# Fewer adaLN blocks in the last group of down-projections, and a joint visit of the value products and the reciprocal broadcasts

## The chip, the cores and the metric

One NeuronCore of a Trainium2 chip runs the whole program. The metric is device time in microseconds, the median of the runs. TensorE (PE) multiplies, VectorE (DVE) and ScalarE (ACT) do the element-wise work, GpSimd (POOL) helps, SyncE (SP) issues most DMAs. Each engine works through its own queue in order; semaphores tie the engines together.

## The reference

One step of a trunk of four layers on 640 tokens (128 of context, 512 latent), width 1024, in fp32. Layer i mixes tokens by kind i mod 3: attention (layers 0 and 3), a Conformer convolution (layer 1), a gated linear attention, GLA (layer 2). A gated ConvFFN with 2816 hidden channels follows in every layer. Each sub-layer is an RMSNorm with shift, scale and gate from `silu(cond) @ mod_w + mod_b`, one set for the context tokens and one for the latent ones:

```
sh1, sc1, g1, sh2, sc2, g2 = split(silu(cond) @ mod_w[i] + mod_b[i], 6)
x = x + g1 * mixer(rms_norm(x, norm1_g[i]) * (1 + sc1) + sh1)
h = rms_norm(x, norm2_g[i]) * (1 + sc2) + sh2
u = dwconv3(h @ w_up + b_up)                 # a, g = halves of u
x = x + g2 * ((silu(g) * a) @ w_down + b_down)
```

In attention a latent query reads its 8x16 neighbourhood and 256 cached context keys, a context query the 128 context keys; the softmax is divided by its sum at the end, 16 heads of 64.

## The kernel before, in words

**Order.** The program is a list of tasks, each with the weights it needs (`units`). `run` works through it in order, and every engine's queue gets its instructions in that order. `weave(main, extra, rate)` puts further tasks between the main ones: after each main task that has units it adds `rate` to a count, and for each whole 1 it takes one task of `extra`. The count starts at 0 in each call.

**Weights.** `fill` issues the loads on SP into a ring of four tiles of 128x1024. `advance` turns them, half by half, into an upper part (ScalarE, L170) and a lower part (on VectorE in the ConvFFN, L171), into rings of four halves, so about two weights ahead of their use. A unit of kind "m" is no weight for TensorE: when `advance` comes to it, it calls `row_unit` at once. That is one **adaLN block**: two VectorE instructions (L377), which multiply 128 rows of `mod_w` by the two condition vectors and sum, for one of the eight row tiles of one of the six vectors of the next layer. `rows_tasks` lists 24 of them (scale 1, shift 1 and gate 2 of the next layer) for the ConvFFNs of layers 0, 1 and 2. Layer 3 has none.

**Matrix products.** `proj` does per step of k six matmuls (L224 to L229: upper and lower parts, two halves of the tokens). In the middle and at the end it calls `advance`, and after every step `pump`, which lets one step of lane A (every generator in it) and one of lane B (its first generator) issue their work. If a step of lane A says "ax", lane B is left out.

**ConvFFN.** `ffn` has three groups of up-projections (10, 7 and 5 pairs of up tasks), each followed by a group of eight down-projection columns over 8, 7 and 7 chunks of hidden channels (`GRP`). In the last group the evacuations are flushed first, then columns 0 and 1 run interleaved as one task, then columns 2 to 7. Each column ends in `x_update`: VectorE adds the gated result to x (L596), then `fin` writes upper (ScalarE, L263) and lower part (VectorE, L266) of the next layer's input, and squares are summed for its norm (ScalarE L287, GpSimd L289). With the next layer an attention, the latent rows are written in a permuted order. `RATES` are the two weave rates, for the ups and for the downs; the first four up tasks stand ahead of the weave, and in layer 0 four more tasks with units (its own gate 2) are among the first ups.

**Attention.** Per pair of heads three projections (q, k, v, 8 steps each) run through `proj`. Lane A holds their evacuations: `normed` for q and k, `values` for v, which transposes the values into the PSUM banks `SB` and `PB` (L802) and has ScalarE copy them out (L803, L804), and says "ax". Lane B holds `units`, the softmax of a pair: scores into `SB`, exponentials with their sums into R, transposes in `PB` (`trans`), products with the values into `B6` (`pv`, L884), for the context tokens into `PB` (L902). At the end the reciprocals of R are broadcast over partitions by ten products with the identity into `SB` and `PB` (L910), copied out by ScalarE (L913, L914), and multiplied in by VectorE (L920). The next pair's `units` start when its keys are done.

Of the kernel before, what the change touches and what calls it, by code (L numbers as in the profile page):

```python
# [25 lines left out]
P = 128  # L26
NCH = 8
CTX = 128
LAT = 512
TOK = CTX + LAT  # L30
# [7 lines left out]
KA = 5  # L38
MODW = 8
W2 = 2  # L40
RATES = (0.0, 1.3)
GRP = ((0, 8), (8, 15), (15, 22))
EPS = 1e-6
EXPLN = "natural_log_exp_and_others"
# [81 lines left out]
class Trunk:  # L126
# [351 lines left out]
    def ffn(self, layer):  # L478
# [152 lines left out]
        def add_down(q):  # L631
            lo, hi = GRP[q]
            main.append(Task(self.lane_a.drain))
            unit = lambda j: ("w", self.i["w_down"][layer, j, :, lo * P:hi * P])
            if q == 0:
                main.append(Task(prep_gb))
            j0 = 0
            if q == 2:
                main.append(Task(flush))
                if nxt:  # L640
                    main.append(Task(lambda: self.shift_cols(self.mod[(layer + 1) % 2][0][:])))
                j0 = 2
                main.append(Task(lambda *ws: down(ws, [0, 1], q), [unit(0), unit(1)]))
            for j in range(j0, NCH):
                main.append(Task(lambda w, j=j: down([w], [j], q), [unit(j)]))
# [4 lines left out]
        for q, (lo, hi) in enumerate(GRP):  # L650
# [3 lines left out]
            if q == 0:  # L654
                tasks += main[:4]
                main = self.weave(main[4:], early, 0.4)
            tasks += self.weave(main, extra, RATES[0], False)
            main = []
            add_down(q)
            tasks += self.weave(main, extra, RATES[1], q == 2)  # L660
            main = []
# [4 lines left out]
    def attention(self, layer, la):  # L666


        S = type("S", (), {})()
# [37 lines left out]
        def load_bias(p, i):  # L707
            at = S.nb % 2
            S.nb += 1
            self.nc.sync.dma_start(out=S.bias[:, 1 + 2 * at:3 + 2 * at], in_=self.i["bias"][la, p, i])  # L710
            S.at[p, i] = 1 + 2 * at
# [97 lines left out]
        def softmax(sc, st, bias, parts, R):  # L809

            nc = self.nc
            sm = self.sm.next()
            n = sc.shape[-1]
            if bias is not None:
                nc.vector.tensor_tensor_reduce(out=st.rearrange("p (a b) -> p a b", a=2),
                                               in0=sc.rearrange("p (a b) -> p a b", a=2), in1=bias, scale=1.0,
                                               scalar=-3.0e38, op0=ALU.add, op1=ALU.max, accum_out=sm[:, 0:1])
                src = st
            else:
                nc.vector.tensor_reduce(out=sm[:, 0:parts], in_=sc.rearrange("p (a b) -> p a b", a=parts),  # L820
                                        axis=AX_X, op=ALU.max)
                src = sc
            nc.vector.tensor_scalar(out=sm[:, 2:2 + parts], in0=sm[:, 0:parts], scalar1=-1.0, scalar2=None,  # L823
                                    op0=ALU.mult)
            w = n // parts
            for a in range(parts):
                nc.scalar.activation(out=st[:, a * w:a * w + w], in_=src[:, a * w:a * w + w], func=AF.Exp,  # L827
                                     bias=sm[:, 2 + a:3 + a], accum_out=R[:, a:a + 1])

        def units(p):  # L830

            nc = self.nc
            b = S.bufs[p]
            Q, K, V, Vc = b["Q"], b["K"], b["V"], b["Vc"]
            sts, pts = {}, {}
            R = S.R.next()

            def scores(n):
                st = self.T.next()[:, 0:512]
                sts[n] = st  # L840
                if n == 8:
                    sc = S.SB[:, 0:256]
                    for hd in range(2):
                        o = KH * hd + 896
                        for part in range(2):
                            nc.tensor.matmul(sc[:, P * hd:P * hd + P], Q[:, hd, part, 0:CTX], K[:, o:o + P],
                                             start=(part == 0), stop=(part == 1))
                    softmax(sc, st[:, 0:256], None, 2, R[:, 8:10])
                else:
                    i, hd = n // 2, n % 2  # L850
                    o = KH * hd
                    sc = S.SB[:]
                    s = 256 + P * i
                    rhs = K[:, o:o + 2 * s].rearrange("p (a b) -> p a b", a=2)[:, :, 0:256]
                    q0 = CTX + P * i
                    nc.tensor.matmul(sc, Q[:, hd, 0, q0:q0 + P], rhs, start=True, stop=False)
                    nc.tensor.matmul(sc, Q[:, hd, 1, q0:q0 + P], rhs, start=False, stop=True)
                    at = S.at[p, i] + hd
                    softmax(sc, st[:], S.bias[:, 0:at + 1:at], 1, R[:, n:n + 1])

            def finish(n):
                if n < 8 and n % 2 == 1:
                    i = 4 * p + n // 2 + 2
                    if i < 4 * NCH:
                        load_bias(i // 4, i % 4)

            def trans(n):
                st, pt = sts.pop(n), S.PT.next()
                m = 2 if n == 8 else 4
                for c in range(m):  # L870
                    nc.tensor.transpose(S.PB[:, P * c:P * c + P], st[:, P * c:P * c + P], self.ident[:])
                if n % 2:
                    nc.vector.tensor_copy(out=pt[:, 0:P * m], in_=S.PB[:, 0:P * m])
                else:
                    nc.scalar.copy(out=pt[:, 0:P * m], in_=S.PB[:, 0:P * m])
                pts[n] = pt

            def pv(i):
                a, c = pts.pop(2 * i), pts.pop(2 * i + 1)
                blocks = (Vc[:, 0], Vc[:, 1], V[:, 1 + i], V[:, 1 + (i + 1) % 4])  # L880
                for k in range(4):
                    for hd, pt in ((0, a), (1, c)):
                        r = slice(64 * hd, 64 * hd + 64)
                        nc.tensor.matmul(S.B6[r, P * i:P * i + P], blocks[k][:, r], pt[:, P * k:P * k + P],  # L884
                                         start=(k == 0), stop=(k == 3))

            for n in range(12):
                if n >= 5 and n % 2 == 1:
                    while "ready" not in b:
                        yield  # L890
                    pv((n - 5) // 2)
                if n < 9:
                    scores(n)
                    finish(n)
                    yield
                if 2 <= n <= 10:
                    trans(n - 2)
                    yield
            pt = pts.pop(8)
            for hd in range(2):  # L900
                r = slice(64 * hd, 64 * hd + 64)
                nc.tensor.matmul(S.PB[r, 256:384], V[:, 0, r], pt[:, P * hd:P * hd + P], start=True, stop=True)  # L902
            oc = S.oT[:, p, 0:CTX]
            nc.scalar.copy(out=oc, in_=S.PB[:, 256:384])
            nc.vector.reciprocal(out=R[:], in_=R[:])
            yield
            for n in range(10):
                a, r = P * (n // 2), slice(64 * (n % 2), 64 * (n % 2) + 64)
                o = S.SB[r, a:a + P] if n < 8 else S.PB[r, 0:P]
                nc.tensor.matmul(o, R[:, n:n + 1].to_broadcast([P, 64]), self.ident[:], start=True,  # L910
                                 stop=True)
            rb = self.acc
            nc.scalar.copy(out=rb[:, 0:512], in_=S.SB[:])  # L913
            nc.scalar.copy(out=rb[:, 512:TOK], in_=S.PB[:, 0:P])  # L914
            yield "ax"
            o = S.oT[:, p]
            for dst, src, rs in ((o[:, CTX:CTX + 448], S.B6[:, 64:512], rb[:, 64:512]),
                                 (o[:, CTX + 448:TOK], S.B6[:, 0:64], rb[:, 0:64]),
                                 (oc, oc, rb[:, 512:640])):
                nc.vector.tensor_tensor(out=dst, in0=src, in1=rs, op=ALU.mult)  # L920
# [907 lines left out]
```

## Time and profile before

| | |
|---|---|
| median of 3 runs | 3404.09 us (3400.82 to 3404.28) |
| profiled execution | 3398.13 us, of which the span is 3396.3 us |
| mean granted TensorE clock | 0.993 |
| TensorE busy | 97% of the span |
| VectorE, ScalarE, GpSimd busy | 64%, 49%, 19% |
| DMA | 352.82 MB, mean 104 GB/s |

Busy shares are means over stages with different limits. TensorE's matmuls are pipelined, so starts of successive instructions tell the pace, and a busy engine may still be slow.

### The profile page before, as it was taken

How to read it: one execution, taken by the hardware profiler on the slowest of the kernel's cores; microseconds unless marked ns; L12 is line 12 of the kernel's file. 1: busy time of each engine (PE TensorE's matmuls, PEld its weight loads, DVE VectorE, ACT ScalarE, POOL GpSimd, SP SyncE). 2: the span in 40 equal slices, each digit the busy share in tenths (PEclk: the TensorE clock that was granted, in tenths of full speed). 3: DMA queues.
4: the chain of work that ended last, by engine and by line, in shares of the span. 5: the costliest groups of instructions: out<-in, count | busy, mean ns of one | idle time of the engine just before them, and what ended most of it. 6: DMA issues, size and time to landing. Idle time of an engine off the chain costs nothing.

```text
span 3396.3 us, 57835 instructions
## 1 busy us (share of the span) xinstructions
PE 3283.8 (97%) x23258; PEld 3091.9 (91%) x23258; DVE 2172.3 (64%) x3674; ACT 1661.6 (49%) x3194; POOL 661.3 (19%) x600
## 2 busy tenths in 40 slices
PE   6999999999999899999999999999999999999999
PEld 4888899999977799999988899999988888999999
DVE  4555666677667767676666676767665556664654
ACT  5666554343413455343455545534456665554432
POOL 4444310000145200000233441000024443200000
PEclk9999999999999899999999999999999999999999
DMA  6333223424365222433332223243333333222222
GB/s 217 114 114 114 78 94 119 131 84 125 100 177 163 71 89 87 125 98 106 115 105 83 91 64 95 87 125 100 104 108 112 109 112 92 76 75 75 70 76 73
DMA packets 111357, 352.82 MB, mean 104 GB/s; under 512 B 14544, under 2 KB 19728, under 8 KB 110704
## 3 DMA queue, kind: packets, MB, share of 16 engines
q1 hardware_dynamic: 107856, 340.15, 32.5%
q0 software_dynamic: 2848, 8.27, 0.7%
q8 instruction: 183, 3.00, 0.4%
q10 hardware_dynamic: 384, 0.69, 0.1%
q14 instruction: 86, 0.70, 0.1%
HBM read 332.28 MB, written 5.77 MB: 100 GB/s over the span
## 4 chain that ended last, share of the span: by engine, by line
PE 57%; DVE 6%; ACT 4%; issue 1%; POOL 1%; DVEq 0%; ACTq 0%; POOLq 0%
PE mm L224 6%; PE mm L228 6%; PE mm L226 6%; PE mm L229 6%; PE mm L227 6%; PE mm L225 6%; PE ax L228 2%; PE ax L224 2%; PE ax L226 2%; PE ax L227 2%; PE ax L229 2%; PE ax L225 2%; PE at L1476 1%; ACT Q L777 1%; PE ob L884 1%
## 5 line engine op out<-in xcount | busy, mean ns | idle before, releaser
L170 ACT CAST wh<-wr 128x512 fp32r<-128x512 f32 (+2 forms) x802 | 469.8, 597 | 525.1 <-PE mm L227 229.4
L171 DVE TENSOR_TENSOR wl<-wr,wh 128x512 fp32r<-128x512 f32 (+1 forms) x555 | 384.8, 702 | 500.9 <-ACT wh L170 499.9
L224 PE MATMUL mm<-xh,wh 128*128 128x320 f32 x1791 | 592.7, 331 | 5.6 <-ACT wh L170 3.1
L228 PE MATMUL mm<-xh,wl 128*128 128x320 f32 x1791 | 557.5, 311 | 4.0 <-POOL wl L171 4.0
L226 PE MATMUL mm<-xl,wh 128*128 128x320 f32 x1791 | 556.1, 311 | 3.5 <-DVE xl L266 2.4
L227 PE MATMUL mm<-xl,wh 128*128 128x322 f32 (+1 forms) x1791 | 557.8, 311 | 0.0
L229 PE MATMUL mm<-xh,wl 128*128 128x322 f32 (+1 forms) x1791 | 556.3, 311 | 0.0
L225 PE MATMUL mm<-xh,wh 128*128 128x322 f32 (+1 forms) x1791 | 555.6, 310 | 0.0
L171 POOL TENSOR_TENSOR wl<-wr,wh 128x512 fp32r<-128x512 f32 (+2 forms) x247 | 321.2, 1306 | 591.6 <-ACT wh L170 497.4
L224 PEld LDWEIGHTS mm<-xh,wh 128*128 128x128 f32 x1791 | 338.3, 189 | 62.0 <-issue 42.3
L225 PEld LDWEIGHTS mm<-xh,wh 128*128 128x128 f32 x1791 | 341.6, 191 | 5.9
L228 PEld LDWEIGHTS mm<-xh,wl 128*128 128x128 f32 x1791 | 338.2, 189 | 4.8 <-POOL wl L171 4.8
L226 PEld LDWEIGHTS mm<-xl,wh 128*128 128x128 f32 x1791 | 337.5, 188 | 5.0 <-DVE xl L266 3.5
L229 PEld LDWEIGHTS mm<-xh,wl 128*128 128x128 f32 x1791 | 341.1, 190 | 0.0
L289 POOL TENSOR_TENSOR acc<-acc,T 128x640 f32<-128x640 f32 x40 | 65.2, 1629 | 1416.5 <-ACT T L287 1397.7
L227 PEld LDWEIGHTS mm<-xl,wh 128*128 128x128 f32 x1791 | 339.3, 189 | 0.0
L517 ACT ACTIVATE U<-T,D 128x128 f32<-128x128 f32 x176 | 71.1, 404 | 532.9 <-DVE D L516 532.9
L377 DVE CUSTOM_DVE_ANT_0 junk<-wr,condb,modb 128x1024 bf16<-128x1024 f32 x144 | 184.5, 1281 | 2.9
L827 ACT ACTIVATE T<-T,sm 128x512 f32<-128x512 f32 x128 | 92.7, 724 | 148.6 <-DVE sm L823 148.3
L526 ACT ACTIVATE y<-U,ffc 128x641 f32<-128x641 f32 x176 | 161.8, 919 | 0.0
L529 DVE SCALAR_TENSOR_TENSOR y<-U,ffc,y 128x641 f32<-128x641 f32 x176 | 156.2, 888 | 7.1
L528 DVE SCALAR_TENSOR_TENSOR y<-U,ffc,y 128x641 f32<-128x641 f32 x176 | 156.2, 887 | 3.6
(381 smaller groups left out, 7581.7 us busy)
## 6 DMA issues: line engine op xcount, KB each, us to landing
wr<-in_w_up SPq DMA_DIRECT2D x176, 512.0 KB, 3.6
wr<-in_mod_w SPq DMA_DIRECT2D x120, 512.0 KB, 3.8
wr<-in_mod_r SPq DMA_DIRECT2D x72, 512.0 KB, 3.6
wr<-in_w_down SPq DMA_DIRECT2D x64, 448.0 KB, 3.3
wr<-in_w_qkv SPq DMA_DIRECT2D x48, 512.0 KB, 4.6
bias<-in_bias SPq DMA_DIRECT2D x64, 256.0 KB, 2.6
wr<-in_w_down SPq DMA_DIRECT2D x32, 512.0 KB, 3.6
cr<-cu SPq DMA_DIRECT2D x120, 84.0 KB, 3.0
```

What stands on the lines that cost most here:

```text
L170: self.nc.scalar.copy(out=h, in_=src[:, a:a + n])
L171: self.lo_eng[self.turn % len(self.lo_eng)].tensor_tensor(out=l, in0=src[:, a:a + n], in1=f32(h), op=ALU.subtract)
L224: mm(oa, wh, ha, start=st, stop=False)
L225: mm(ob, wh, hb, start=st, stop=False)
L226: mm(oa, wh, la, start=False, stop=False)
L227: mm(ob, wh, lb, start=False, stop=False)
L228: mm(oa, wl, ha, start=False, stop=en)
L229: mm(ob, wl, hb, start=False, stop=en)
L377: nc.vector.tensor_tensor_reduce(out=self.junk, in0=w, in1=self.condb[:, g], scale=1.0, scalar=self.modb[:, layer, v, j:j + 1], op0=ALU.mu ...
L526: nc.scalar.activation(out=y[:], in_=u[:, 1:642], func=AF.Identity, scale=c[:, 2:3], bias=c[:, 4:5])
L528: stt(out=y[:], in0=u[:, 0:641], scalar=c[:, 1:2], in1=y[:], op0=ALU.mult, op1=ALU.add)
L529: stt(out=y[:], in0=u[:, 2:643], scalar=c[:, 3:4], in1=y[:], op0=ALU.mult, op1=ALU.add)
```

## The change

The weave rates go from 0 and 1.3 to 0.12 and 1.25, so that up tasks take a block now and then. In attention the reciprocal is issued one lane step earlier, ahead of the transposes of the context scores. The broadcasts follow the value products in the same step, in place of one step later. Their last part moves from columns 0 to 127 of `PB` to columns 384 to 511, and ScalarE's copy of the context values is issued behind the broadcasts.

```diff
--- before.py
+++ after.py
@@ -38,7 +38,7 @@
 KA = 5
 MODW = 8
 W2 = 2
-RATES = (0.0, 1.3)
+RATES = (0.12, 1.25)
 GRP = ((0, 8), (8, 15), (15, 22))
 EPS = 1e-6
 EXPLN = "natural_log_exp_and_others"
@@ -889,10 +889,14 @@
                     while "ready" not in b:
                         yield
                     pv((n - 5) // 2)
+                    if n == 11:
+                        break
                 if n < 9:
                     scores(n)
                     finish(n)
                     yield
+                if n == 10:
+                    nc.vector.reciprocal(out=R[:], in_=R[:])
                 if 2 <= n <= 10:
                     trans(n - 2)
                     yield
@@ -900,18 +904,15 @@
             for hd in range(2):
                 r = slice(64 * hd, 64 * hd + 64)
                 nc.tensor.matmul(S.PB[r, 256:384], V[:, 0, r], pt[:, P * hd:P * hd + P], start=True, stop=True)
-            oc = S.oT[:, p, 0:CTX]
-            nc.scalar.copy(out=oc, in_=S.PB[:, 256:384])
-            nc.vector.reciprocal(out=R[:], in_=R[:])
-            yield
             for n in range(10):
                 a, r = P * (n // 2), slice(64 * (n % 2), 64 * (n % 2) + 64)
-                o = S.SB[r, a:a + P] if n < 8 else S.PB[r, 0:P]
+                o = S.SB[r, a:a + P] if n < 8 else S.PB[r, 384:512]
                 nc.tensor.matmul(o, R[:, n:n + 1].to_broadcast([P, 64]), self.ident[:], start=True,
                                  stop=True)
-            rb = self.acc
+            rb, oc = self.acc, S.oT[:, p, 0:CTX]
+            nc.scalar.copy(out=oc, in_=S.PB[:, 256:384])
             nc.scalar.copy(out=rb[:, 0:512], in_=S.SB[:])
-            nc.scalar.copy(out=rb[:, 512:TOK], in_=S.PB[:, 0:P])
+            nc.scalar.copy(out=rb[:, 512:TOK], in_=S.PB[:, 384:512])
             yield "ax"
             o = S.oT[:, p]
             for dst, src, rs in ((o[:, CTX:CTX + 448], S.B6[:, 64:512], rb[:, 64:512]),
```

## Rows read from the trace of the kernel before

**Rows 1.** Page, busy time by engine: us, share, instructions.

```profile
PE 3283.8 (97%) x23258; PEld 3091.9 (91%) x23258; DVE 2172.3 (64%) x3674; ACT 1661.6 (49%) x3194; POOL 661.3 (19%) x600
```

**Rows 2.** Windows, L224, six last columns, layers 0-3: length, busy (count), clock, DMA.

```profile
877.75:920.53 42.78, 13.47 (x43) 8.16 (x43) 0.96 0.39 117
1630.06:1672.83 42.77, 13.47 (x42) 8.14 (x43) 0.96 0.39 116
2478.47:2524.34 45.87, 13.54 (x42) 8.20 (x43) 0.96 0.34 108
3354.78:3391.75 36.97, 12.92 (x42) 7.73 (x42) 1.00 0.26 88
```

**Rows 3.** Chain of waits, last down groups, layers 1, 2: start, us, what.

```profile
1630.11 1.28 DVE junk L377
...
1632.72 0.93 DVE x L596 x2
...
1640.14 1.20 DVE junk L377
...
1647.69 1.20 DVE junk L377
...
2490.16 1.20 DVE junk L377
...
2498.48 1.20 DVE junk L377
```

**Rows 4.** Windows, L224, two steps each.

```profile
883.03:887.82 4.79, 0.72 (x2) 0.37 (x3) 1.00 0.13 53
1635.34:1640.42 5.08, 0.72 (x2) 0.49 (x3) 0.89 0.11 46
2483.74:2490.45 6.71, 0.73 (x3) 0.50 (x3) 0.91 0.07 30
1640.42:1643.22 2.80, 0.94 (x2) 0.54 (x3) 0.59 0.54 164
```

**Rows 5.** Timeline, TensorE, layer 1: start, us, instruction [idle before <-releaser].

```profile
1638.06 0.42 PE L224 MATMUL mm<-f,wh 128*128 128x320 f32 x1 [1.67 <-ACT wh L170]
```

**Rows 6.** Page, costliest groups; windows, ups of layer 1: PE, PEld, DVE, ACT, POOL.

```profile
L377 DVE CUSTOM_DVE_ANT_0 junk<-wr,condb,modb 128x1024 bf16<-128x1024 f32 x144 | 184.5, 1281 | 2.9
...
1210.00:1330.00 120.00, 120.00 (x813) 120.00 (x812) 80.83 (x124) 59.84 (x100) 0.00 (x0) 1.00 0.24 75
```

**Rows 7.** Timeline, TensorE, attention of layer 3, end of a pair.

```profile
2803.28 0.39 PE L902 MATMUL pb<-PT,V 128*64 128x128 f32 x4
...
2803.60 0.41 PE L224 MATMUL mm<-xh,wh 128*128 128x320 f32 x1
...
2804.59 0.27 PE L802 MATMUL sb<-ident,A 128*128 128x128 f32 x1
...
2805.05 0.39 PE L224 MATMUL mm<-xh,wh 128*128 128x320 f32 x1
...
2806.12 1.09 PE L910 MATMUL sb<-ident,R 128*64 128x128 f32 x16
...
2807.04 0.39 PE L910 MATMUL pb<-ident,R 128*64 128x128 f32 x4
...
2807.36 0.41 PE L224 MATMUL mm<-xh,wh 128*128 128x320 f32 x1
...
2808.34 0.31 PE L224 MATMUL mm<-xh,wh 128*128 128x320 f32 x1
```

**Rows 8.** Timeline, ScalarE, there; waits before and for L910: us, times.

```profile
2807.26 0.59 ACT L913 COPY acc<-sb 128x512 f32<-128x512 f32 x1 [0.70 <-PE sb L910]
2807.74 0.27 ACT L914 COPY acc<-pb 128x128 f32<-128x128 f32 x1
...
  ACT V L804: 2.7, 14
...
  ACT acc L913: 13.4, 16
```

## The prediction

> **What bounds the kernel now.** The page comes first: TensorE is busy for 3283.8 of the 3396.3 us span, so only what TensorE waits for, or does in a slower way, can be saved [rows 1]. I then looked for stretches in which it does the same work in different times. The last group of down-projections is the same in every layer: after the first two columns come six more, each 7 steps of k, 42 steps of six matmuls. In layer 3, which has no following layer, they take 36.97 us, or 0.88 us a step. In layers 0, 1 and 2 they take 42.78, 42.77 and 45.87 us [rows 2]. The reader is to see 42 (or 43) matmuls of L224 in all four rows: 5.81 + 5.80 + 8.90 = 20.5 us are lost without any work being added on TensorE.
>
> The chain of waits says to whom. In layer 1 it leaves TensorE and runs through VectorE: a block of `row_unit` (L377), the update of x (L596), and, after the lower halves of the next weights, the next block [rows 3]. TensorE's own timeline agrees: it waited 1.67 us for a weight's upper half [rows 5], which ScalarE casts behind the work that hangs on the update of x. In the up-projections TensorE is busy for 120.00 of 120 us, with VectorE at 80.83 [rows 6]. So VectorE binds in three short stretches, and has time to spare elsewhere.
>
> **The change part by part.**
>
> *Which blocks move.* There are 24 blocks for each of three layers. With the old rates the first two down groups take 10 each (8 tasks at 1.3) and the last the remaining 4. With 0.12 and 1.25 the down groups still take 10 each. The ups take 1, 1 and 1 (16, 14 and 10 tasks; in layer 0 the first has 20 unit tasks, so 2). That leaves 0 blocks in layer 0's last group and 1 in those of layers 1 and 2: 4 + 3 + 3 = 10 blocks move, each with its 512 KB load on SP's queue. The one that stays is the first, ahead of the pair of columns, where TensorE has 14 steps of work to cover it.
>
> *What leaves the last group.* A block is two L377 of 1281 ns [rows 6]. In layer 1 the second block starts at 1630.11 and the update of x behind it at 1632.72 [rows 3]. VectorE would do that update at once, since both columns' matmuls are issued by 1630.06, the start of the stretch in [rows 2]. So all that hangs on it comes 2.6 us earlier: the cast, the upper half, the lower half. Around that wait and the one for the lower half behind it two steps took 4.79, 5.08 and 6.71 us in layers 0, 1 and 2 [rows 4] where two plain ones take 1.76: losses of 3.03, 3.32 and 4.95 us. Take 2.6 us from each, and 0.43, 0.72 and 2.35 us remain: 3.5 us.
>
> The rest, 20.5 - 11.3 = 9.2 us, is the steps at a low clock that follow, and the waits two and three columns on. From block to block layer 1's VectorE takes 1647.69 - 1640.14 = 7.55 us, layer 2's 2498.48 - 2490.16 = 8.32 us [rows 3]. Without the 2.6 us of a block that is 5.0 and 5.7 us, against 6.16 us that TensorE needs for a column. So VectorE no longer binds, though in layer 2 by only 0.4 us, and the later waits go. Saved: 20.5 - 3.5 = 17.0 us. Bounds: 9.2 us if the first waits stay whole, 20.5 us if all go. What is late next is the cast behind the update of x for the second of the two columns, in layer 2 above all, whose rows are permuted and so written in more pieces.
>
> *The clock.* Behind those waits the granted clock was 0.59 for 2.80 us (two steps, 1.04 us more than plain) [rows 4], part of the 9.2 us. [...]
>
> *What the ups take on.* VectorE is free there for 39 us of 120, 2.3 us in each of the 17 units [rows 6]. A block of 2.6 us is absorbed in a little over one unit. It stands in VectorE's queue behind the lower halves of weights that are used two units later, and ahead of an evacuation for which three PSUM tiles give room. I take 0; the cover is this lead of two units. If it were gone, ten blocks would cost up to 26 us. Nothing below zero is excluded by a row, but TensorE is already busy throughout, so a gain is. DMA is busy for 0.24 of that stretch [rows 6], so the moved loads fit; SP's queue merely issues one load in three groups of ups that it issued later before. The last of them lies two to three units ahead of the flush at the end of the ups, and its 2.6 us should have drained by then.
>
> *Attention.* Per pair of heads (8 pairs, 2 layers) lane B's visits to TensorE were: last value products, a step of the projection, the value transposes of lane A, a step, the broadcasts, a step, a step. Their steps are 0.99, 1.07 and 0.98 us [rows 7], and 0.88 us for one with no visit on either side [rows 2]. With the broadcasts behind the value products a step follows the joint visit and leads to the transposes (0.99), one follows these (0.98 like that behind the broadcasts), and two are plain: 0.99 + 0.98 + 0.88 + 0.88 = 3.73 against 0.99 + 1.07 + 0.98 + 0.88 = 3.92 us. Saved 0.19 a pair, 3.0 us in 16. The four matmuls of L902 took 0.32 us where those of L910 take 0.92 / 16 = 0.06 each [rows 7]; if that tail is shared too, 0.09 more, 4.5 us in all. The next pair gains no earlier start, as it waits for its keys. The reciprocal goes one step ahead, behind VectorE work of the same lane; its result is wanted two visits later.
>
> The new wait: the transposes write the banks that ScalarE copies out after the broadcasts. L913 began 1.14 us after the first broadcast, L914 0.48 us later, and took 0.27 us [rows 7, 8]: done 1.89 us after the first broadcast. The transposes come 0.92 + 0.32 + 0.98 = 2.22 us after it. ScalarE waited for TensorE there, not the reverse, and behind these copies stand only casts of keys. I take no wait, and 0 to 4.5 us for the part.
>
> A second reading of the 1.07: weight loads of the broadcasts waited 2.7 us in 14 pairs, 0.19 each, for the copy of V [rows 8]. [...]
>
> *Sum.* 17.0 + 3.0 - 0 = 20 us. The profiled execution took 3398.13 us (span 3396.3, 1.8 around it) and would take 3378. The median of the runs is 3404.09, 6 us above it, and I forecast against that: 3384 us.
>
> **The rivals.**
> 1. *The first waits stay.* The update of x is not what the upper half waits for, but ScalarE's own queue of casts. For: the wait names ScalarE [rows 5]. Against: the chain goes on from it to VectorE and the block. Then 9.2 + 3.0: 3392 us.
> 2. *Attention gives nothing*, as the broadcasts' only recorded wait is for the copy of V [rows 8], not the reciprocal, and the transposes take it over: 3387 us.
> 3. *The ups feel the blocks*: four of ten in full, 10.5 us: 3394 us. Against: TensorE's 120.00 [rows 6].
> 4. *Slower: the transposes wait for ScalarE in every pair.* If ScalarE starts the three copies 2.5 us later than above, behind its casts of keys, TensorE waits 2.2 us in each of 16 pairs: 35 us, the 3.0 are lost, and the time is 3422. It outweighs the rest from a wait of 17 / 16 = 1.1 us. For: these banks make TensorE wait for ScalarE now. Against: ScalarE stood waiting before L913 in all 16 pairs, 13.4 us in all [rows 8].
> 5. *Neither part does what it says*: the blocks only look like the cause, and the following stage absorbs the gain. Around 3402 us. Against: layer 3, without blocks, loses nothing [rows 2].
>
> **How the numbers follow.** Forecast 0.60 (own range 3378 to 3390), rivals 0.12, 0.14, 0.07, 0.03 and 0.04. 0.2% is 6.8 us, about what a measurement of this kernel can tell from no change: faster means below 3397. Forecast and rivals 1 to 3 are faster, 0.93; I give 0.90, since rivals 1 and 3 together or a high median would come near the bound. 0.06 for the same, 0.04 for slower. The range, 3374 to 3396, holds the forecast with both ends of attention and of the last group, and rivals 1 to 3.
>
> **What would show it.** Right: no L377 in the last group of layer 0 and two in those of layers 1 and 2; the six columns at 37 to 38 us in layers 0 and 1 and 39 to 40 in layer 2; TensorE still busy throughout the ups; broadcasts right behind L902, and steps of 0.99, 0.98 and 0.88 after them. Wrong: the six columns near 41 us, a wait of L802 for ScalarE in each pair, or new waits for L171 in the ups.

## The result, and the profile after

The changed kernel takes 3383.96 us (median of six runs, 3380.8 to 3385.41); the kernel before, on the same chips, 3401.8 us (six runs, 3397.26 to 3404.28). The ratio is 0.9947, with a 95% interval of 0.9936 to 0.9957; between the medians that is 17.8 us faster. The forecast was 3384.0 us.

The profiled execution took 3385.29 us (span 3383.5). This is its first row; the busy time of TensorE fell by 6.5 us against [rows 1], and the rest of the 12.8 us by which the span fell (3396.3 to 3383.5) is idle time that is gone. That execution lies 1.3 us above its median and the one of before 3.7 us below its own, so the two spans show 5 us less than the medians.

```profile
PE 3277.3 (97%) x23258; PEld 3089.8 (91%) x23258; DVE 2165.4 (64%) x3674; ACT 1657.8 (49%) x3194; POOL 659.9 (20%) x600
```

The windows over L224 for the six last columns, layers 0 to 3, as in [rows 2] (length, TensorE busy, weight loads busy, granted clock, DMA):

```profile
877.09:914.56 37.47, 12.94 (x42) 7.87 (x43) 1.00 0.29 84
1627.68:1665.16 37.48, 13.00 (x42) 7.91 (x43) 1.00 0.32 93
2472.70:2513.38 40.68, 13.46 (x42) 8.15 (x43) 0.96 0.29 85
3341.97:3378.93 36.96, 12.91 (x42) 7.72 (x42) 1.00 0.25 88
```

Against the 36.96 us of layer 3 the first three now lose 0.51, 0.52 and 3.72 us, 4.75 in all where it was 20.5. The same two steps as in [rows 4], then the first step of layer 2 right behind them:

```profile
882.37:884.64 2.27, 0.62 (x2) 0.37 (x3) 1.00 0.00 0
1632.96:1635.24 2.28, 0.61 (x2) 0.38 (x3) 1.00 0.00 0
2477.98:2481.92 3.94, 0.72 (x2) 0.38 (x3) 1.00 0.00 0
...
2481.92:2483.47 1.55, 0.42 (x1) 0.31 (x2) 0.52 0.49 49
```

In layers 0 and 1 nothing is late beyond these two steps. In layer 2 two waits remain, and TensorE works on at a granted clock of 0.52: that step takes 1.55 us, where a plain one takes 0.88. Its timeline there names the two waits; [rows 5], the wait of 1.67 us in layer 1, is gone.

```profile
2479.77 0.41 PE L224 MATMUL ax<-f,wh 128*128 128x320 f32 x1 [0.74 <-ACT wh L170]
2481.53 0.41 PE L228 MATMUL ax<-f,wl 128*128 128x320 f32 x1 [0.92 <-DVE wl L171]
```

VectorE's blocks in the last groups are one in layer 1 (below, the first of its two L377), one in layer 2 (from 2468.66) and none in layer 0:

```profile
1623.63 1.27 DVE L377 CUSTOM_DVE_ANT_0 junk<-wr,condb,modb 128x1024 bf16<-128x1024 f32 x1
```

The first ups of layer 1, as in [rows 6], still keep TensorE busy from end to end:

```profile
1207.00:1327.00 120.00, 120.00 (x813) 120.00 (x812) 82.46 (x128) 60.69 (x101) 0.00 (x0) 1.00 0.26 78
```

The place where the moved blocks do cost something is the flush behind each layer's last ups. TensorE goes on with the first pair of down columns, and in its tenth step it waits, before as after, in layers 0 to 2, for the first upper half that ScalarE casts behind the flush (the second half of column 1's weight). This is the wait of layer 0 after, 0.88 and 0.90 us in layers 1 and 2:

```profile
872.26 0.42 PE L224 MATMUL mm<-f,wh 128*128 128x320 f32 x1 [0.89 <-ACT wh L170]
```

and this is layer 0 before, where it is 0.57 us (0.58 in layers 1 and 2):

```profile
872.92 0.41 PE L224 MATMUL mm<-f,wh 128*128 128x320 f32 x1 [0.57 <-ACT wh L170]
```

Attention of layer 3, the end of the same pair as in [rows 7]: the broadcasts (L910) stand right behind the last value products (L906, which was L902 before). The step that starts at 2793.32 takes 0.99 us up to the transposes (L802), those at 2794.83 and 2795.80 take 0.97 and 0.87 us.

```profile
2791.91 0.39 PE L906 MATMUL pb<-PT,V 128*64 128x128 f32 x4
2792.13 1.04 PE L910 MATMUL sb<-ident,R 128*64 128x128 f32 x16
2793.01 0.39 PE L910 MATMUL pb<-ident,R 128*64 128x128 f32 x4
2793.32 0.41 PE L224 MATMUL mm<-xh,wh 128*128 128x320 f32 x1
2794.31 0.27 PE L802 MATMUL sb<-ident,A 128*128 128x128 f32 x1
...
2794.83 0.39 PE L224 MATMUL mm<-xh,wh 128*128 128x320 f32 x1
2795.80 0.30 PE L224 MATMUL mm<-xh,wh 128*128 128x320 f32 x1
2796.67 0.31 PE L224 MATMUL mm<-xh,wh 128*128 128x320 f32 x1
```

ScalarE there, as in [rows 8]: it still stands waiting for TensorE before its copies, and the last one, which empties the bank that four of the five transposes write, ends at 2794.08 + 0.28 = 2794.36. TensorE's first weight load for these four (PEld, below) starts at 2794.42, right behind it. No idle time is listed for this load, but by the trace it waits for ScalarE's semaphore, and before the change it started together with the first transpose. The transposes' visit takes 2794.83 - 2794.31 = 0.52 us, where it took 2805.05 - 2804.59 = 0.46 [rows 7].

```profile
2793.44 0.27 ACT L913 COPY oT<-pb 128x128 f32<-128x128 f32 x1 [1.33 <-PE pb L910]
...
2794.08 0.28 ACT L915 COPY acc<-pb 128x128 f32<-128x128 f32 x1
...
2794.42 0.42 PEld L802 LDWEIGHTS pb<-ident,A 128*128 128x128 f32 x4
```

### The profile page after: what moved, and what is told of

Same layout as the page of the kernel before. It is cut to its first block, busy times and chain, and to the rows that moved or that the text cites. A ratio compares the mean times of both kernels' runs of the same rounds, so it can differ in the third digit from the quotient of the medians.

```text
span 3383.5 us, 57817 instructions
## 1 busy us (share of the span) xinstructions
PE 3277.3 (97%) x23258; PEld 3089.8 (91%) x23258; DVE 2165.4 (64%) x3674; ACT 1657.8 (49%) x3194; POOL 659.9 (20%) x600
## 4 chain that ended last, share of the span: by engine, by line
PE 57%; DVE 6%; ACT 4%; issue 2%; POOL 1%; DVEq 0%; ACTq 0%; POOLq 0%
PE mm L224 6%; PE mm L228 6%; PE mm L226 6%; PE mm L229 6%; PE mm L227 6%; PE mm L225 6%; PE ax L228 2%; PE ax L224 2%; PE ax L226 2%; PE ax L229 2%; PE ax L227 2%; PE ax L225 2%; PE at L1477 1%; ACT Q L777 1%; PE ob L884 1%
## 5 line engine op out<-in xcount | busy, mean ns | idle before, releaser
L171 DVE TENSOR_TENSOR wl<-wr,wh 128x512 fp32r<-128x512 f32 (+1 forms) x555 | 383.0, 703 | 483.4 <-ACT wh L170 482.8
L224 PE MATMUL mm<-xh,wh 128*128 128x320 f32 x1791 | 591.3, 330 | 5.7 <-ACT wh L170 3.1
L171 POOL TENSOR_TENSOR wl<-wr,wh 128x512 fp32r<-128x512 f32 (+2 forms) x247 | 321.0, 1305 | 589.8 <-ACT wh L170 494.1
L224 PEld LDWEIGHTS mm<-xh,wh 128*128 128x128 f32 x1791 | 338.3, 189 | 59.8 <-issue 40.6
L289 POOL TENSOR_TENSOR acc<-acc,T 128x640 f32<-128x640 f32 x40 | 65.2, 1629 | 1399.0 <-ACT T L287 1385.4
L377 DVE CUSTOM_DVE_ANT_0 junk<-wr,condb,modb 128x1024 bf16<-128x1024 f32 x144 | 184.7, 1282 | 3.0
```

The costliest lines, as they stand in the source:

```text
L171: self.lo_eng[self.turn % len(self.lo_eng)].tensor_tensor(out=l, in0=src[:, a:a + n], in1=f32(h), op=ALU.subtract)
L224: mm(oa, wh, ha, start=st, stop=False)
L377: nc.vector.tensor_tensor_reduce(out=self.junk, in0=w, in1=self.condb[:, g], scale=1.0, scalar=self.modb[:, layer, v, j:j + 1], op0=ALU.mu ...
```

## The experiments

The theory: the last groups were slow because blocks stood ahead of the update of x, and attention gains one visit per pair. The rivals: the attention part gives all of the gain or nothing; the ups take back part of what the last groups give; the clock decides layer 2. Ratios are to the kernel before on the same chip, with 95% intervals. Its median was 3401.0 us (16 runs) beside the first four kernels and 3402.86 us (10 runs) beside the last four; each kernel ran five to eleven times. "Loses" is time above the 36.96 us of layer 3, in layers 0, 1 and 2.

### One part alone: rates

```
 RATES = (0.12, 1.25)      # new; attention as before
```

> The kernel before with the new weave rates alone; attention as it was. Theory (VectorE's queue in the last down groups holds TensorE up): the six last columns at about 37.5, 37.5 and 40.7 us in layers 0 to 2, as with the whole change, and 14.5 to 16 us less than before in all; attention at its old pace, its steps around the broadcasts at 0.99, 1.07 and 0.98 us. Rival (ScalarE's casts hold it, or the stage that follows takes the gain back): under 9 us less. From two profiled executions the Conformer and GLA layers seemed to give back 3.3 and 1.4 us after the change; if that comes of starting earlier, they do so here too; if it is the spread of single executions, this profile shows another value.

Measured: 3384.99 us, 0.9957 (0.9945 to 0.997), about 15 us. The rates carry most of the gain. The last groups lose 0.51, 0.53 and 2.19 us. Layer 2 is the telling one: TensorE had the same two waits (0.74 and 0.93 us) in the same two steps (3.95 us), and then ran at the full clock:

```profile
2481.79:2485.30 3.51, 1.24 (x4) 0.74 (x5) 1.00 0.44 131
```

So the 1.54 us by which the changed kernel's layer 2 is worse than this one's is the clock alone, and it comes or stays away behind equal waits. Three more kernels of this section have these two waits (rates of 0.2, layer 0's blocks elsewhere, and the late reciprocal: 0.72 to 0.74 and 0.91 to 0.92 us), and all three lose 2.2 us there, as this one does, without the 1.5 us more. So the slow stretch came in one of five traces. What decides that is not shown.

The expectation also asked whether the layers behind give time back. From the last downs of layer 0 to the first downs of layer 1 the trace of before took 419.60 us, the changed kernel's 3.26 us more, this one 0.53 more, and the other kernels' 1.35 to 6.77 more, the one without new rates among them (1.99). In the next such stretch, with the GLA, all traces take 1.6 us or more above that of before, that kernel's too, which starts no earlier. It is thus the spread of single executions, not an answer to the change, and its 3.26 + 1.59 = 4.9 us in the profiled pair are about what the two spans show less than the medians.

### One part alone: attention

```
 RATES = (0.0, 1.3)        # old; attention as after
```

> The changed kernel with the old weave rates, so the attention part alone. Theory: 0.18 us less per pair and 3.0 us less in 16 pairs, of which the seventh pair of each layer gives some back, as the broadcasts there wait for the reciprocal: 2 to 3 us less than before in all. The last down groups as before: 42.8, 42.8 and 45.9 us for the six last columns. Rival (the transposes of the values take the wait over): 0 to 1.6 us less, with waits of L802 for ScalarE.

Measured: 3398.06 us, 0.9995 (0.9986 to 1.0004). By the ratio that is 1.7 us, between the medians 2.9 us, and by the time alone it is not told apart from nothing. The traces tell it: taken from pair to pair over the same 24 steps, the twelve steady pairs in layers 0 and 3 took 0.14 to 0.22 us less each than in the trace of before. In the changed kernel eleven did so by 0.15 to 0.21, and one in layer 3 took 0.2 us more: TensorE waited 0.46 us there for VectorE's work on the scores (L815). The seventh pair differs between single executions by 1 to 2 us either way, whatever the kernel (its waits for the softmax are older than the change), and nothing is read from it here.

### No block in the last ups and the last downs

```
-RATES = (0.12, 1.25)
+RATES = (0.2, 1.25)
```

> The changed kernel with rates 0.2 and 1.25: no adaLN block in the last down group of any layer, and none in the last group of up-projections. After the change TensorE's wait at the flush ahead of the last down group had grown by 0.32 us in each of layers 0 to 2. Theory (the block moved into the last ups has not drained from VectorE's queue by the flush): that wait falls back from 1.05 to 0.73 us in all three layers, 1 us less than the changed kernel in all; the first block of layers 1 and 2 was covered by the pair of columns, so the six columns stay as in the changed kernel. Rival (the flush waits for something else that the new rates moved): 1.05 us stays. Second theory on the same run: five or six blocks in the first two groups of ups leave TensorE there without a wait; the rival says that it shows waits for L171 there.

Measured: 3389.13 us, 0.9968 (0.9957 to 0.998), slower than the changed kernel's ratio, the intervals just touching. In layers 1 and 2 it did what was meant: the wait behind the flush is back at the old length, and these last groups lose 0.53 and 2.18 us. The ups, with five or six blocks in their first two groups, take the same times as before within 0.02 us. Layer 0 spoilt it. TensorE's timeline at the start of its last downs:

```profile
873.32 0.63 PE L224 MATMUL mm<-f,wh 128*128 128x320 f32 x1 [7.71 <-ACT wh L170]
...
879.70 0.31 PE L224 MATMUL mm<-f,wh 128*128 128x320 f32 x1
```

A wait of 7.71 us, then four steps in 879.70 - 873.32 = 6.38 us instead of 3.52, their matmuls mostly 0.27 us apart instead of 0.15. Here TensorE stops in the second step of the pair of columns, eight steps earlier than in the changed kernel. Both kernels cast their last two halves ahead of the flush at about the same time (ScalarE's timeline, this kernel first, then the changed one):

```profile
859.71 1.02 ACT L170 CAST wh<-wr 128x512 fp32r<-128x512 f32 x2
```

```profile
859.56 1.02 ACT L170 CAST wh<-wr 128x384 fp32r<-128x384 f32 x2
```

But here they are the first and second half of column 0's weight (512 and 384 wide). There they are the second half of column 0's and the first of column 1's, as column 0's first half had been cast with the pair before, at 853.68. So the look-ahead is one half shorter, and column 1's first half is cast only behind the flush. By the code, a block's load takes one of the four raw weight tiles, and falling between certain units of layer 0's own stream it shortens the look-ahead; that this is how it comes about is argued, not shown, but nothing in the ups wins the half back.

### The same, with layer 0's blocks elsewhere

```
+RATES = (0.2, 1.25)
+ ... self.weave(main, extra, (0.0, 0.3, 0.0)[q] if layer == 0 else RATES[0], False)
```

> As the run with rates 0.2 and 1.25, except that layer 0 takes no block in its first group of ups (where its own gate 2 brings weight units of another kind), four in the second and none in the third. In the run before this, layer 0's TensorE waited 7.7 us at the head of the last down group, and 11 us were lost there. Theory (a block between two such units takes the ring of four raw tiles, the casts fall from four halves ahead to two and never catch up, so at the flush the first cast stands behind all evacuations): that wait goes back to 0.58 us in layer 0 too, and the kernel is 8 to 11 us faster than with plain 0.2 and 1.25; the flush waits are 0.73 us in all of layers 0 to 2, so 1 us less than the changed kernel. Rival (the wait comes of leaving the last groups without a block, which then change the order of the loads): it stays.

Measured: 3382.95 us, 0.9943 (0.9931 to 0.9956). With layer 0's blocks kept out of its first ups (four stand in the second) the 7.71 us are gone. The wait behind the flush in layer 0:

```profile
874.39 0.41 PE L224 MATMUL mm<-f,wh 128*128 128x320 f32 x1 [0.58 <-ACT wh L170]
```

Layers 1 and 2 wait 0.58 us too. So where a block falls in layer 0 causes the long wait, and a block in the last ups causes the extra 0.3 us. Of the 1 us by which this kernel was to beat the changed one the time shows nothing clear of its interval, and the trace has a reason: in layer 0's second downs two blocks now stand in a row (four L377, from 764.65 to 769.84), TensorE waits behind them for a lower half, and that group takes 2.85 us longer than before.

```profile
770.59 0.42 PE L228 MATMUL mm<-f,wl 128*128 128x320 f32 x1 [1.55 <-DVE wl L171]
```

### What still waits in layer 2

In the changed kernel the squares of column 1, the second of the pair, and their sum (L287 on ScalarE, L289 on GpSimd) are issued right behind that column's update, ahead of the weight that TensorE waits for. Here they are issued one column later, ahead of the update of column 2:

```
-        self.square(j)
+        if sq:
+            self.square(j)
...
-                    self.fin(j, self.A[0], nperm)
+                    self.fin(j, self.A[0], nperm, j != 1)
...
+                if q == 2 and nxt and js[0] == 2:
+                    self.square(1)
                 x_update(pm, js[0], q)
```

> The changed kernel with one edit: in the last down group the squares of column 1 (ScalarE L287, GpSimd L289) are issued ahead of the update of x of column 2, and no longer right behind column 1, where they stand ahead of the casts for column 3. Theory (what is left of the wait for column 3's weights is ScalarE's 0.72 us for the squares ahead of the cast, and GpSimd's sum, during which VectorE's lower half takes 1.5 to 1.7 us in place of 0.69): the waits of 0.25 us in layers 0 and 1 go, those of 0.74 and 0.92 us in layer 2 and the low clock behind them go too; 0.5, 0.5 and up to 3.7 us less, 3 to 4.7 us less than the changed kernel in all. Rival (the cast waits for the rows of column 1 itself): layer 2 keeps over 2 us of its loss, and under 1.5 us is gained. A second rival: the later sum meets column 4's lower half in its place, and nothing is gained.

Measured: 3380.07 us, 0.9943 (0.993 to 0.9955). By the ratios that is 1.4 us less than the changed kernel, where 3 to 4.7 us were expected, and the intervals don't part the two; the traces do. Last groups, layers 0 and 2 (36.96 us in layer 1 too):

```profile
876.80:913.76 36.96, 12.92 (x42) 7.85 (x43) 1.00 0.29 84
...
2471.69:2509.55 37.86, 13.11 (x42) 7.93 (x43) 1.00 0.30 91
```

Layers 0 and 1 lose nothing now, layer 2 0.90 us, and no clock falls: 4.75 - 0.90 = 3.9 us less than in the changed kernel's trace, of which 1.5 us are the clock that fell in that one. In the changed kernel ScalarE, GpSimd and VectorE met in layer 2 like this:

```profile
2478.48 0.72 ACT L287 ACTIVATE T<-x 128x640 f32<-128x640 f32 x1
2479.11 1.02 ACT L170 CAST wh<-wr 128x512 fp32r<-128x512 f32 x2
2479.29 1.64 POOL L289 TENSOR_TENSOR acc<-acc,T 128x640 f32<-128x640 f32 x1 [434.26 <-ACT T L287]
2479.75 2.20 DVE L171 TENSOR_TENSOR wl<-wr,wh 128x512 fp32r<-128x512 f32 x2 [0.18 <-ACT wh L170]
```

and here the casts stand ahead of the square, and the two lower halves take 1.16 us instead of 2.20, as GpSimd's sum starts only at 2479.22. The one edit moves both, the square ahead of the casts and the sum beside the lower halves, so what each is worth is read from these rows alone:

```profile
2477.48 1.02 ACT L170 CAST wh<-wr 128x512 fp32r<-128x512 f32 x2
2478.40 0.73 ACT L288 ACTIVATE T<-x 128x640 f32<-128x640 f32 x1
2478.48 1.16 DVE L171 TENSOR_TENSOR wl<-wr,wh 128x512 fp32r<-128x512 f32 x2
```

### Both

> The run on the lead and the one on the deferred squares together: no block in the last ups or the last down group, and column 1's squares ahead of column 2's update. If both theories hold their gains add: 1 us and 3.9 us less than the changed kernel, 22 to 24 us less than the kernel before, 3378 to 3380 us. If the block that is gone from the last ups had covered something, only the 3.9 us show.

The last two edits together: 3381.46 us, 0.9938 (0.9924 to 0.9951), the lowest ratio of all, though no interval parts it from the changed kernel's: 21 us less than before, where 22 to 24 were expected. The last groups lose 0, 0 and 0.87 us, and TensorE waits 0.58 us behind each flush. The two blocks in a row in layer 0 remain, and their 2.85 us are more than the 0.9 us that the flushes give back, so in the traces this kernel's ConvFFNs save 16.8 us, those of the kernel with deferred squares alone 18.8.

### More blocks in the last group

```
-RATES = (0.0, 1.3)
+RATES = (0.0, 1.2)       # kernel before: 6 blocks in each last group, not 4
```

> The kernel before with down rates of 1.2 in place of 1.3: six blocks per layer in the last down group, not four, one after each of its first six tasks. Theory (VectorE is the bound of that group, so each further block there costs its own 2.6 us): the six last columns take 5.2 us more in each of layers 0 to 2, 15.6 us more in all, less up to 1 us a column in which layers 0 and 1 still have room: 11 to 16 us slower than before. Rival (ScalarE's casts are the bound and the blocks only stand beside them): under 4 us slower.

Measured: 3412.71 us, 1.0031 (1.0019 to 1.0042): slower, by some 10 us. The last groups of layers 0 and 2, against [rows 2] (45.57 us in layer 1):

```profile
879.57:925.44 45.87, 13.77 (x42) 8.22 (x43) 0.96 0.44 131
...
2493.77:2543.86 50.09, 14.04 (x42) 8.45 (x43) 0.93 0.40 120
```

That is 3.1, 2.8 and 4.2 us more, 10.1 in all, for two more blocks in each: 1.7 us a block, where four cost 20.5 / 12 = 1.7 us each. The expectation, 2.6 us for each and 11 to 16 us in all, was too high, and its rival (under 4 us) fell: the price follows the blocks, at less than VectorE's own time for one. The second downs, with one block fewer, take 0.5 us less in each layer.

### The reciprocal back behind the value products

```
-                if n == 10:
-                    nc.vector.reciprocal(out=R[:], in_=R[:])
...
+            nc.vector.reciprocal(out=R[:], in_=R[:])
             for n in range(10):
```

> The changed kernel with the reciprocal back between the context products and the broadcasts, so the joint visit without the early reciprocal. Theory (the gain is the visit that is saved; the early reciprocal is what lets it go without a wait): in the six plain pairs of each layer VectorE reaches the reciprocal about when TensorE reaches the broadcasts, and TensorE waits 0 to 0.3 us per pair for it: 0 to 4 us slower than the changed kernel. Rival (the early reciprocal is what the part gains by, since the broadcasts waited for it before): the whole 3 us of the attention part are lost and more, each L910 waits for VectorE. In the seventh pair, where the early reciprocal was late by 0.3 to 0.4 us in the changed kernel, the wait is the same or longer.

Measured: 3390.68 us, 0.9966 (0.9954 to 0.9979), 6.5 us above the changed kernel's ratio. The visit in the pair shown above:

```profile
2794.23 0.39 PE L904 MATMUL pb<-PT,V 128*64 128x128 f32 x4
2794.53 1.09 PE L909 MATMUL sb<-ident,R 128*64 128x128 f32 x16
...
2795.77 0.41 PE L224 MATMUL mm<-xh,wh 128*128 128x320 f32 x1
```

From the value products to the next step it takes 1.54 us, where the changed kernel takes 2793.32 - 2791.91 = 1.41. The broadcasts wait for the reciprocal here too, though no idle time of TensorE is listed: their first weight load starts right behind it.

```profile
2794.25 0.22 DVE L905 RECIPROCAL R<-R 128x10 f32<-128x10 f32 x1
...
2794.52 0.20 PEld L909 LDWEIGHTS sb<-ident,R 128*64 128x64 f32 x4
```

So it is, by 0.12 us each, in ten of the fourteen pairs that are not the seventh of their layer; in the other four the reciprocal ends before the value products do, and the visit takes 1.41 us. In the seventh pair of both layers the broadcasts wait for the reciprocal in earnest. The first row is this kernel's, the second the changed kernel's (total us, times, longest):

```profile
PE sb L909 <- DVE R L905: 3.1, 2, 2.3
```

```profile
PE sb L910 <- DVE R L899: 0.7, 2, 0.4
```

Of the steady pairs all but one gain only 0.03 to 0.18 us over before. The rows so give 10 x 0.12 + 3.1 - 0.7 = 3.6 us of the 6.5; the rest is within the two intervals. The expected 0 to 4 us more than the changed kernel hold by these rows, not by the ratio. This kernel is no faster than the one with the rates alone (0.9957): the early reciprocal is a condition of the attention gain, not a detail of it.

## Why the prediction was right

*The last groups, 17.0 us forecast.* The profiles give 20.5 - 4.75 = 15.7 us; the kernel with the rates alone, whose clock did not fall, 20.5 - 3.23 = 17.3. Rival 1 fell: the first waits went with the blocks, in layers 0 and 1 to 0.5 us where 0.43 and 0.72 were forecast. Layer 2 was to be at 39 to 40 us and is at 40.68, while the four other kernels with the same two waits there are at 39.1. What was named as late next is what is late, the cast behind the update of the second column, but its second half had been missed: GpSimd's sum beside VectorE's lower halves, which the rows of the experiment that defers the squares show.

*The clock.* The low clock was to go with the waits, as part of the 9.2 us. In layers 0 and 1 it did: the granted clock is 1.00 over their six columns. In layer 2 it fell to 0.52 behind waits of 0.74 and 0.92 us. Behind the same waits the kernel with the rates alone kept 1.00, and three others lost 2.2 us there, as it did, so these waits alone do not tell it beforehand.

*The ups, 0 us forecast.* Wrong by 0.9 us. The step that failed is "its 2.6 us should have drained by then". VectorE's timeline for the last ups of layer 0 after, with the evacuations L515 that open its work on each unit:

```profile
842.18 0.83 DVE L515 TENSOR_TENSOR T<-ax,rstd 128x642 f32<-128x642 f32 x1
845.47 1.28 DVE L377 CUSTOM_DVE_ANT_0 junk<-wr,condb,modb 128x1024 bf16<-128x1024 f32 x1
...
851.13 0.82 DVE L515 TENSOR_TENSOR T<-mm,rstd 128x642 f32<-128x642 f32 x1
857.52 0.82 DVE L515 TENSOR_TENSOR T<-mm,rstd 128x642 f32<-128x642 f32 x1
863.80 0.82 DVE L515 TENSOR_TENSOR T<-ax,rstd 128x642 f32<-128x642 f32 x1
```

They are 8.95, 6.39 and 6.28 us apart. Before, they are 7.10 apart:

```profile
857.36 0.83 DVE L515 TENSOR_TENSOR T<-mm,rstd 128x642 f32<-128x642 f32 x1
864.46 0.83 DVE L515 TENSOR_TENSOR T<-ax,rstd 128x642 f32<-128x642 f32 x1
```

Behind the block VectorE wins back 0.7 to 0.8 us a unit, and two units don't suffice: 0.32 us are left at the last L515, from which everything up to that upper half follows, and TensorE waits 0.3 us longer, in three layers. The figure of 2.3 us free in each unit was an average over VectorE's total; the chain of evacuation, convolution and product leaves only a third of it to catch up with. The kernels without that block are back at 0.57 to 0.58 us. Rival 3, a cost of 10 us in the ups, did not come.

*Attention, 3.0 us forecast.* The time of its part alone gives 2.9 us between the medians and 1.7 by the ratio, with an interval that holds nothing too; the steady pairs give 0.14 to 0.22 us each where 0.19 was forecast. The second reading puts the 1.07 down to the wait for the copy of V, and the 0.09 us above 0.98 would then have moved to the transposes. It fell: no step of 1.07 is left. The sum was right for partly the wrong reason. The tail of the value products is shared after all (0.22 us to the first broadcast instead of 0.32, and 0.88 to the last four instead of 0.92), and the steps save 0.21 us. From the value products to the last plain step the pair shown so saves 0.30 us, the transposes' 0.06 us already off. Then one step between the next pair's first scores took 0.10 us more (1.69 for 1.59), in every steady pair: VectorE starts on these scores (L815) 0.14 us behind their end, where before it was 0.04; what holds it is not shown.

"I take no wait" for the transposes was wrong by a little. The working had the last copy done 1.89 us after the first broadcast, 0.33 us ahead of the transposes, from the two copies of before. It left out that the copy of the context values now stands ahead of these two in ScalarE's queue: the last copy ends 2794.36 - 2792.13 = 2.23 us after the first broadcast, and the transposes begin at 2.18. So the lead was gone, in 14 of the 16 pairs, but the price was 0.06 us a pair and 0.7 us in all, not the 1.1 us a pair from which rival 4 outweighs the rest. Rivals 2 and 4 fell by the size of this wait, not for want of it, and that the copies come no later than this was not foreseen. A second wait was added in the seventh pair, for the reciprocal, 0.7 us in all.

*The sum.* 15.7 - 0.9 + 2.9 = 17.7 us, against 17.8 us between the medians. That it fits so well is luck too: the first term is 17.3 where the clock does not fall, and the last 1.7 by the ratio. The forecast took 20 us off 3404.09; with six runs the kernel before lies at 3401.8, and the forecast time came out to the microsecond because a saving 2 us too large was taken from a median 2 us too high.

## What to carry to other kernels

When an engine has spare time on average, look for the places where it has none, and compare the same stretch of work with and without the suspected work beside it; here one layer without it gave the price of 1.7 us a block before anything was built. Work that is moved into slack needs more than slack: measure how much of the lag the chain there wins back per unit, and keep the last units ahead of a flush free. A wait too short to be listed as idle time shows when the first instruction starts just behind the one that releases it, and in the length of the same visit before and after. Where a ring of buffers carries two streams, a moved load can shorten the look-ahead of the other for good.

## What the runs showed of the hardware

- VectorE's subtraction of 128x512 (L171) takes 0.69 us alone. With GpSimd adding a 128x640 tile beside it, one took 1.73 us in layer 2 of the changed kernel (1.66 in layers 0 and 1), and two took 2.20 instead of 1.16. GpSimd ended at 2479.29 + 1.64 = 2480.93, 1.18 us after the first of the two had begun, and they were 1.04 us late. So in 1.18 us beside GpSimd VectorE lost 1.04; why is not shown.
- The same two waits within two steps (0.72 to 0.74 and 0.91 to 0.93 us) stand in five traces, each of another kernel. In one a granted clock of 0.52 followed, and the group lost 3.72 us; in four it lost 2.2 us, with a clock of 1.00 in the one with the rates alone. A wait of 7.71 us was followed by four steps in 6.38 us instead of 3.52.
- Two visits of TensorE to another lane, joined, cost less than their sum: 1.41 us for value products and broadcasts back to back, where they took 0.32 and 1.24 us apart. With the reciprocal issued between them the joint visit took 1.54 us in ten of fourteen pairs, as the first weight load of the broadcasts starts 0.05 us behind the reciprocal's end.
